# The address offset between activations and weight buffers in a two-layer decoder kernel: 112 bytes for every activation slot

## The chip, the cores and the metric

The kernel runs on one core of a Trainium2 chip. The metric is device time in microseconds for one execution. A core has a matrix engine (PE; its weight loads are listed apart as PEld), a vector engine (DVE), a scalar engine (ACT), a general engine (POOL) and queues that issue transfers (SP). All tiles below lie in the core's on-chip memory, which has 128 partitions; an address is a byte position inside a partition.

## What is computed

A decoder trunk of two layers over 256 tokens with model width 2048. Cut to its lines of work:

```
u = rms_norm(h, mix_norm[0]);  q, f, i, g = split(u @ w_a_in, 4)       # layer 0: gated linear recurrence
h += (head_norm(recurrence(q, f, i)) * silu(g)) @ w_a_out
u = rms_norm(h, mix_norm[1]);  q = u @ w_b_q                           # layer 1: forgetting attention
h += (softmax(q k^T / sqrt(d) + D_t - D_s) v) @ w_b_out
# behind the mixer of either layer:
h += relu(rms_norm(h, mlp_norm) @ w_up)**2 @ w_down                    # d_ff = 8192
h += (p @ w_ple_up) * sigmoid(rms_norm(h, ple_norm) @ w_ple_gate)
# behind layer 0: k, v, f = split(rms_norm(h, kv_norm) @ w_kvf)
out = rms_norm(h, final_norm)
```

Everything is float32. Nearly all of the work is matrix products of 256 tokens with weights of 2048 rows.

## The kernel before

**Precision.** A float32 number is split into two numbers of the matrix engine's single-pass float32 format: a high part (a rounding copy) and a low part (the rest). A product is three matmuls: high weight with high activation, high weight with low activation, low weight with high activation.

**Weights.** `load_slab` (L78) brings 1 MB of weights into one of three `raw` buffers, with a transfer issued from the SP queue. ACT writes the high parts into one of four `whi` buffers (L92), DVE the low parts into one of four `wlo` buffers (L93). A `whi` or `wlo` buffer is 4096 bytes a partition.

**Two kinds of product.** In `mm_split` (L105, called by `mm_tile`) the weights are the stationary operand, a block of 128x128, and the activations are the moving operand, 256 columns: L111, L112 and L113 are its three matmuls, and 16 steps over the contraction make 48 matmuls for an output block `ps`. In `mm_tokens` (L116) it is the other way round: a block of activations is stationary and 512 or 416 columns of weights move (L130 to L132). It serves only the values of the recurrence (stationary `u_a`, 512 columns) and the values of the attention (stationary `u_kv`, 416 columns).

**Activations.** They live in three large slots, each with 16 x 2 x 256 float32 a partition: 16 blocks of the contraction, high and low part, 256 tokens. A step of the contraction is 2048 bytes and a part 1024 bytes, so all blocks of a slot start at the same place modulo 256 bytes. A step in the weight buffers is 512 bytes. `shifted` (L68) allocates a slot a little larger than needed and begins the data some elements into it. The embeddings' tile `pt` is made by the same helper. Who uses which slot, in the order of the program:

| slot | tiles |
|---|---|
| A | `u_a`, `hid` of layer 0 in chunks 0 and 2, `u_kv`, `u_m` of layer 1, `u_p` of layer 1 |
| B | `o_a`, `hid` of layer 0 in chunks 1 and 3, `u_q`, `hid` of layer 1 in chunks 0 and 2 |
| C | `u_m` and `u_p` of layer 0, `o_b`, `hid` of layer 1 in chunks 1 and 3 |

**Stages, in order of time.** Recurrence: `u_a` with the weights of forget gate, query and gate, and small matmuls for each of 16 heads between blocks of 48. Output projection: `o_a`. MLP: `up(0)`, then `up(b)`, `down(b-1)` for four chunks b, each with 16 blocks of 48, that is 768 matmuls; `up` moves `u_m`, `down` moves `hid`. Embedding stage (`ple`): 16 blocks with `u_p`, and 6 matmuls with `pt` for each. Then the attention with `u_kv` (values, keys) and `u_q` (queries), its projection with `o_b`, and MLP and embedding stage again. A framework puts the instructions of an engine in order from the program's text and a simulated timeline, and an allocator gives the addresses.

Of the kernel before, what the change touches and what calls it, by code (L numbers as in the profile page):

```python
# [11 lines left out]
F32R = mybir.dt.float32r  # L12
# [6 lines left out]
P = 128  # L19
T = 256  # L20
D = 2048
KC = D // P
# [12 lines left out]
def yoco_kernel(ctx, tc, a, out):  # L35
    nc = tc.nc
    big = ctx.enter_context(tc.tile_pool(name="big", bufs=1))
# [27 lines left out]

    h = big.tile([P, KC, T], F32, name="h", tag="h")

    def shifted(pool, kc, name, tag, bufs=None):  # L68

        n = kc * 2 * T  # L70
        t = pool.tile([P, n + 16], F32R, name=name, tag=tag, bufs=bufs or 1)
        return t[:, 12 : 12 + n].rearrange("p (k w t) -> p k w t", w=2, t=T)

    def slot(which, name):
        return shifted(big, KC, name, "slot" + which)


    def load_slab(src, n, parts, before=None):  # L78

        raw = wp.tile([P, D], F32, name="raw", tag="raw", bufs=3)  # L80
        m = n // parts
        if not before:
            nc.sync.dma_start(raw[:, :n], src)
        got = []
        for i in range(parts):
            r = raw[:, i * m : (i + 1) * m]
            if before:
                before[i]()
                nc.sync.dma_start(r, src[:, i * m : (i + 1) * m])
            hi = wp.tile([P, 1024], F32R, name="whi", tag="whi", bufs=4)  # L90
            lo = wp.tile([P, 1024], F32R, name="wlo", tag="wlo", bufs=4)
            nc.scalar.copy(hi[:, :m], r)  # L92
            nc.vector.tensor_tensor(lo[:, :m], r, hi[:, :m].bitcast(F32), op=ALU.subtract)  # L93
            got.append((hi, lo))
        return got
# [4 lines left out]
    def mm_tile(src, act, kcs=KC):  # L100

        pairs = load_slab(src, kcs * P, 2 if kcs > 8 else 1)
        return mm_split(pairs, act, kcs)

    def mm_split(pairs, act, kcs=KC, off=0):  # L105
        ps = psm.tile([P, T], F32, name="ps", tag="mm")
        for k in range(kcs):
            kk = k + off
            pair, kl = pairs[kk // 8], kk % 8
            st, sp = k == 0, k == kcs - 1  # L110
            nc.tensor.matmul(ps, wk(pair, kl, 0), act[:, k, 0, :], start=st, stop=False)  # L111
            nc.tensor.matmul(ps, wk(pair, kl, 0), act[:, k, 1, :], start=False, stop=False)  # L112
            nc.tensor.matmul(ps, wk(pair, kl, 1), act[:, k, 0, :], start=False, stop=sp)  # L113
        return ps
# [70 lines left out]
    def plain_split(dst, k, src):  # L185
        nc.scalar.copy(dst[:, k, 0, :], src)
        nc.vector.tensor_tensor(dst[:, k, 1, :], src, dst[:, k, 0, :].bitcast(F32), op=ALU.subtract)
# [11 lines left out]
    def mlp(layer, u, stats, slots, u2, g2, pool):  # L199
# [3 lines left out]
        def up(b):  # L203
            hid[b] = slot(slots[b % 2], f"hid{layer}_{b}")
            for n in range(KC):
                ps = mm_tile(a["w_up"][layer, b * KC + n], u)
                if not rs:
                    rs.append(stats.rstd())
                t = pool.tile([P, T], F32, name="up", tag="up", bufs=2)
                nc.vector.scalar_tensor_tensor(t, ps, 0.0, rs[0], op0=ALU.max, op1=ALU.mult)  # L210
                s = pool.tile([P, T], F32, name="hsq", tag="hsq", bufs=2)
                nc.scalar.activation(s, t, AF.Square)
                plain_split(hid[b], n, s)
# [18 lines left out]
    def ple(layer, u, stats, after, pool):  # L232

        praw = pool.tile([P, 2, T], F32, name="praw", tag="praw", bufs=1)
        nc.gpsimd.dma_start(praw, a["pT"][layer])
        pt = shifted(pool, 2, "pt", "pt")
        for k in range(2):
            plain_split(pt, k, praw[:, k, :])
        rstd = None
        wu = None  # L240
        for n in range(KC):
            if n % 8 == 0:
                wu = load_slab(a["w_pu"][layer, n // 8], D, 2)
            pu = mm_split(wu, pt, kcs=2, off=2 * (n % 8))
            up = pool.tile([P, T], F32, name="up", tag="up", bufs=2)
            nc.scalar.copy(up, pu)
            last = layer == 1 and n == KC - 1
            ps = mm_tile(a["w_pg"][layer, n], u)
            rstd = rstd or stats.rstd()
            t = pool.tile([P, T], F32, name="gate", tag="gate", bufs=2)  # L250
            nc.vector.tensor_tensor(t, ps, rstd, op=ALU.mult)
            s = pool.tile([P, T], F32, name="sig", tag="sig", bufs=2)
            nc.scalar.activation(s, t, AF.Sigmoid)
            if last:

                nc.scalar.activation(scrap, s[:, 0:1], AF.Sqrt)
            nc.vector.tensor_tensor(up, up, s, op=ALU.mult)
            nc.vector.tensor_tensor(h[:, n, :], h[:, n, :], up, op=ALU.add)
            after(n)
# [14 lines left out]
    nc.vector.tensor_scalar(nomlb, omlb, -1.0, None, op0=ALU.mult)  # L274

    u_a = slot("A", "u_a")
    o_a = slot("B", "o_a")
    with tc.tile_pool(name="hg", bufs=2) as hp, tc.tile_pool(name="hps", bufs=1, space=PSUM) as hps:

# [251 lines left out]
    late = ctx.enter_context(tc.tile_pool(name="late", bufs=1))  # L531

    def slotc(name):
        return shifted(late, KC, name, "slotC")

    _slot = slot

    def slot(which, name):
        return slotc(name) if which == "C" else _slot(which, name)
# [21 lines left out]
    def after0(n):  # L561
        scaled_split(u_kv, n, G_KV)
        scaled_split(u_q, n, G_MIX + 1)
        st_kv.add(n)

    ple(0, up_(), stats, after0, mp)
    mctx.__exit__(None, None, None)

# [130 lines left out]
    def after1(n):  # L699
        st_f.add(n, n == KC - 1)  # L700
        nc.scalar.activation(h[:, n, :], h[:, n, :], AF.Copy, scale=gains[:, G_FIN, n : n + 1])

    ple(1, up_(), stats, after1, mp)
    rstd = st_f.rstd()
    k = 0
# [69 lines left out]
```

## Time and profile before

| | |
|---|---|
| time, median of 3 runs | 2541.58 us (2541.26 to 2541.87) |
| profiled execution | 2541.92 us, of which its span is 2539.8 us |
| granted clock of the matrix engine | 0.998 |
| busy: PE, DVE, ACT, POOL | 99%, 62%, 51%, 1% |
| matmuls in the profile | 20808 |
| weights and other data read | 464.35 MB, 184 GB/s over the span |

The span runs from the first to the last instruction; about 2 us of the time lie outside it. A matmul's recorded duration is longer than the distance to the next one, since matmuls are pipelined: where the text speaks of the pitch, it is that distance, from start to start, found as the length of a stretch divided by its number of matmuls. In tables by stretches each row gives start and end, then the length, then for each engine busy time and number of instructions; PEclk is the granted clock as a share of full speed.

### The profile page before, as it was taken

The page shows a single profiled execution, that of the slowest core. Times are in us where ns is not written, and L with a number is a line of the kernel's source. Part 1 is how long each engine was busy: PE and PEld are TensorE (multiplying, and loading weights), DVE is VectorE, ACT ScalarE, POOL GpSimd, SP SyncE. Part 2 cuts the span into 40 slices and gives each one's busy share as a digit, 9 for nine tenths or more (in the row PEclk, how much of TensorE's full clock was granted, in tenths as well). Part 3 has the DMA queues.
Part 4 walks back from the last instruction along what each step waited for, and adds up shares of the span by engine and source line. Part 5 has one row for each costly group of instructions (what it writes and reads, how often), then busy time and mean ns, then how long its engine had stood idle before and what let it go on. Part 6 is the DMA issues. An engine that isn't in the chain of part 4 may idle for free.

```text
span 2539.8 us, 48653 instructions
## 1 busy us (share of the span) xinstructions
PE 2523.9 (99%) x20808; PEld 2501.8 (99%) x20808; DVE 1569.9 (62%) x2350; ACT 1284.7 (51%) x1966; POOL 23.8 (1%) x71
## 2 busy tenths in 40 slices
PE   9999999999999999999999999999999999999997
PEld 8999999999999999999999999999999999999997
DVE  8787787655545555556774566665555555555665
ACT  7665565545434434445654555555443443444554
POOL 1000000000000000000000000000000000000000
PEclk9999999999999999999999999999999999999999
DMA  6455455555555555555555555555555555555553
GB/s 250 166 175 188 170 174 196 191 190 185 183 183 186 196 187 190 188 183 198 185 175 191 192 172 172 179 189 185 183 185 198 184 185 190 190 184 199 183 183 117
DMA packets 68505, 469.62 MB, mean 185 GB/s; under 512 B 7936, under 2 KB 8640, under 8 KB 15040
## 3 DMA queue, kind: packets, MB, share of 16 engines
q1 hardware_dynamic: 66096, 460.88, 52.3%
q0 software_dynamic: 1760, 4.78, 1.0%
q8 instruction: 163, 2.67, 0.4%
q10 hardware_dynamic: 432, 0.85, 0.1%
q14 instruction: 54, 0.44, 0.0%
HBM read 464.35 MB, written 2.13 MB: 184 GB/s over the span
## 4 chain that ended last, share of the span: by engine, by line
PE 99%; ACT 0%; DVE 0%; DMA 0%; SPq 0%; DVEq 0%; issue 0%
PE ps L111 30%; PE ps L112 30%; PE ps L113 30%; PE pst L131 2%; PE pst L132 2%; PE pst L130 2%; PE pa L437 0%; PE pl L638 0%; DMA h<-in_xT 0%; PE ptp L661 0%; DVE h L708 0%; PE ms L474 0%; PE pob L671 0%; PE pb L440 0%; PE po L459 0%; PE pa L439 0%
## 5 line engine op out<-in xcount | busy, mean ns | idle before, releaser
L93 DVE TENSOR_TENSOR wlo<-raw,whi 128x1024 fp32r<-128x1024 f32 (+2 forms) x882 | 1069.2, 1213 | 706.5 <-ACT whi L92 705.3
L92 ACT CAST whi<-raw 128x1024 fp32r<-128x1024 f32 (+2 forms) x882 | 917.6, 1041 | 1157.4 <-PE ps L112 1006.1
L111 PE MATMUL ps<-u_m,whi 128*128 128x256 f32 x2048 | 575.6, 281 | 0.0
L113 PE MATMUL ps<-u_m,wlo 128*128 128x256 f32 x2048 | 575.3, 281 | 0.0
L112 PE MATMUL ps<-u_m,whi 128*128 128x256 f32 x2048 | 575.3, 281 | 0.0
L111 PE MATMUL ps<-hid,whi 128*128 128x256 f32 x2048 | 569.3, 278 | 0.0
L112 PE MATMUL ps<-hid,whi 128*128 128x256 f32 x2048 | 569.3, 278 | 0.0
L113 PE MATMUL ps<-hid,wlo 128*128 128x256 f32 x2048 | 569.3, 278 | 0.0
L112 PEld LDWEIGHTS ps<-u_m,whi 128*128 128x128 f32 x2048 | 384.9, 188 | 0.1
L111 PEld LDWEIGHTS ps<-u_m,whi 128*128 128x128 f32 x2048 | 384.9, 188 | 0.1
L113 PEld LDWEIGHTS ps<-u_m,wlo 128*128 128x128 f32 x2048 | 384.9, 188 | 0.0
L112 PEld LDWEIGHTS ps<-hid,whi 128*128 128x128 f32 x2048 | 384.6, 188 | 0.0
L111 PEld LDWEIGHTS ps<-hid,whi 128*128 128x128 f32 x2048 | 384.6, 188 | 0.0
L113 PEld LDWEIGHTS ps<-hid,wlo 128*128 128x128 f32 x2048 | 384.6, 188 | 0.0
L111 PE MATMUL ps<-u_a,whi 128*128 128x256 f32 x768 | 217.6, 283 | 0.0
L113 PE MATMUL ps<-u_a,wlo 128*128 128x256 f32 x768 | 216.7, 282 | 0.0
L112 PE MATMUL ps<-u_a,whi 128*128 128x256 f32 x768 | 216.1, 281 | 0.0
L111 PEld LDWEIGHTS ps<-u_a,whi 128*128 128x128 f32 x768 | 144.5, 188 | 0.2
L112 PEld LDWEIGHTS ps<-u_a,whi 128*128 128x128 f32 x768 | 144.5, 188 | 0.2
L113 PEld LDWEIGHTS ps<-u_a,wlo 128*128 128x128 f32 x768 | 144.4, 188 | 0.0
L112 PE MATMUL ps<-u_p,whi 128*128 128x256 f32 x512 | 143.7, 281 | 0.0
L111 PE MATMUL ps<-u_p,whi 128*128 128x256 f32 x512 | 143.7, 281 | 0.0
(257 smaller groups left out, 3674.3 us busy)
## 6 DMA issues: line engine op xcount, KB each, us to landing
raw<-in_w_up SPq DMA_DIRECT2D x128, 1024.0 KB, 4.9
raw<-in_w_down SPq DMA_DIRECT2D x128, 1024.0 KB, 4.8
raw<-in_w_ain SPq DMA_DIRECT2D x48, 1024.0 KB, 4.8
raw<-in_w_pg SPq DMA_DIRECT2D x32, 1024.0 KB, 4.9
raw<-in_w_vf SPq DMA_DIRECT2D x20, 832.0 KB, 4.4
raw<-in_w_aout SPq DMA_DIRECT2D x16, 1024.0 KB, 4.7
raw<-in_w_k SPq DMA_DIRECT2D x16, 1024.0 KB, 4.7
raw<-in_w_q SPq DMA_DIRECT2D x16, 1024.0 KB, 6.4
```

The costliest lines, as they stand in the source:

```text
L92: nc.scalar.copy(hi[:, :m], r)
L93: nc.vector.tensor_tensor(lo[:, :m], r, hi[:, :m].bitcast(F32), op=ALU.subtract)
L111: nc.tensor.matmul(ps, wk(pair, kl, 0), act[:, k, 0, :], start=st, stop=False)
L112: nc.tensor.matmul(ps, wk(pair, kl, 0), act[:, k, 1, :], start=False, stop=False)
L113: nc.tensor.matmul(ps, wk(pair, kl, 1), act[:, k, 0, :], start=False, stop=sp)
L130: nc.tensor.matmul(o, act[:, kk, 0, tok], hi, start=st, stop=False)
L131: nc.tensor.matmul(o, act[:, kk, 0, tok], lo, start=False, stop=False)
L132: nc.tensor.matmul(o, act[:, kk, 1, tok], hi, start=False, stop=sp)
```

## The change

All slots and `pt` get more room, and their data begin at another place in it, so that they start 112 bytes past a multiple of 256 bytes counted from the weight buffers.

```diff
-    def shifted(pool, kc, name, tag, bufs=None):
+    def shifted(pool, kc, name, tag, shift):
         n = kc * 2 * T
-        t = pool.tile([P, n + 16], F32R, name=name, tag=tag, bufs=bufs or 1)
-        return t[:, 12 : 12 + n].rearrange("p (k w t) -> p k w t", w=2, t=T)
+        t = pool.tile([P, n + 64], F32R, name=name, tag=tag, bufs=1)
+        return t[:, shift : shift + n].rearrange("p (k w t) -> p k w t", w=2, t=T)
     def slot(which, name):
-        return shifted(big, KC, name, "slot" + which)
+        return shifted(big, KC, name, "slot" + which, 60)
...
-        pt = shifted(pool, 2, "pt", "pt")
+        pt = shifted(pool, 2, "pt", "pt", 28)
...
     def slotc(name):
-        return shifted(late, KC, name, "slotC")
+        return shifted(late, KC, name, "slotC", 28)
```

The shift counts elements of 4 bytes. The addresses of the two programs, as allocated:

| | first byte before | mod 256 | past the weights | first byte after | mod 256 | past the weights |
|---|---|---|---|---|---|---|
| `whi` (4 buffers) | 131456 | 128 | | 131840 | 0 | |
| `wlo` (4 buffers) | 147840 | 128 | | 148224 | 0 | |
| slot A | 32944 | 176 | 48 | 33136 | 112 | 112 |
| slot B | 65776 | 240 | 112 | 66160 | 112 | 112 |
| slot C | 164272 | 176 | 48 | 164720 | 112 | 112 |
| `pt` | 203248 | 240 | 112 | 203888 | 112 | 112 |

"Past the weights" is the difference of the two places modulo 256. The residual stream `h` stays where it was; the constants and the `raw` buffers move up by 384 bytes like the weights, the working tiles of the recurrence too, and those of the MLP and the attention by 576. No instruction is added, removed or moved: on each engine the order, the shapes and the waits are the same in both programs.

## The prediction

> **What bounds the kernel now.** I read the page's busy times and chain first, then the waits of PE.
>
> ```profile
> span 2539.8 us, 48653 instructions
> PE 2523.9 (99%) x20808; PEld 2501.8 (99%) x20808; DVE 1569.9 (62%) x2350; ACT 1284.7 (51%) x1966; POOL 23.8 (1%) x71
> PE 99%; ACT 0%; DVE 0%; DMA 0%; SPq 0%; DVEq 0%; issue 0%
> ```
> ```profile
> PE ps_ssq L161 <- ACT sq L148: 2.4, 1, 2.4
> PE warm L56 <- POOL ones L52: 1.1, 1, 1.1
> PE pst L131 <- DVE wlo L93: 0.8, 2, 0.5
> PE pst L130 <- ACT whi L92: 0.7, 2, 0.5
> ```
>
> The chain of work that ended last is PE for 99% of the span, and the four rows are all that PE waited for: 5.0 us. So the time is the number of matmuls times their pitch, and only a change of the pitch can move it. The next view asks whether the pitch is the same everywhere: the `down` steps of the two MLPs, tile `hid`, one row for each.
>
> ```profile
> core 0: us, PE busy (x) PEld busy (x) DVE busy (x) ACT busy (x), PEclk, DMA share, GB/s
> 673.30:764.20 90.90, 90.89 (x768) 90.84 (x768) 0.42 (x1) 0.41 (x1) 1.00 0.54 186
> 855.10:942.20 87.10, 87.10 (x768) 87.02 (x768) 0.42 (x1) 0.41 (x1) 1.00 0.56 193
> 1033.00:1123.90 90.90, 90.86 (x768) 90.90 (x769) 0.42 (x1) 0.41 (x1) 1.00 0.53 185
> 1123.90:1211.00 87.10, 87.10 (x770) 87.07 (x768) 0.00 (x0) 0.00 (x0) 1.00 0.56 193
> 1884.60:1971.70 87.10, 87.10 (x768) 87.03 (x768) 0.42 (x1) 0.41 (x1) 1.00 0.56 192
> 2062.50:2153.40 90.90, 90.85 (x768) 90.88 (x768) 0.42 (x1) 0.41 (x1) 1.00 0.54 185
> 2244.30:2331.40 87.10, 87.09 (x769) 87.10 (x770) 0.42 (x1) 0.41 (x1) 1.00 0.56 193
> 2331.40:2422.30 90.90, 90.90 (x770) 90.83 (x768) 0.00 (x0) 0.00 (x0) 1.00 0.54 187
> ```
>
> These eight steps do the same work with the same code at the same clock (1.00), yet four take 90.9 us and four take 87.1 us. By the table of slots those of 90.9 us use, in order, A, A, C, C, and those of 87.1 us B each time. A and C begin 48 bytes past the weights, B 112. The pitch is 90.9/768 = 118.4 ns at 48 and 87.1/768 = 113.4 ns at 112: a difference of 3.8 us for 768 matmuls, or 4.95 ns each. The same split shows in the recorded durations of one of the three matmuls by tile (least, median, most; first and last start).
>
> ```profile
> L112 PE MATMUL ps<-u_a,whi x768: 278/281/366, 31.1 to 403.8; 128*128 128x256 f32 x192
> L112 PE MATMUL ps<-u_m,whi x2048: 278/281/283, 491.2 to 2244.1; 128*128 128x256 f32 x187
> L112 PE MATMUL ps<-u_p,whi x512: 278/280/286, 1211.8 to 2524.6; 128*128 128x256 f32 x171
> L112 PE MATMUL ps<-u_kv,whi x256: 278/281/283, 1405.0 to 1601.5; 128*128 128x256 f32 x128
> L112 PE MATMUL ps<-u_q,whi x256: 275/275/281, 1412.2 to 1608.0; 128*128 128x256 f32 x128
> L112 PE MATMUL ps<-o_b,whi x256: 278/280/365, 1609.0 to 1702.2; 128*128 128x256 f32 x128
> ```
>
> Medians of 280 and 281 belong to tiles in A and C, 275 to `u_q`, which lies in B. Nothing else about a tile sorts them: `u_kv` and `u_q` alternate block by block in the same stage and still differ. A and C are far apart (32944 and 164272) and agree.
>
> **The change part by part.** It removes and adds no instruction and changes no wait; every price is a pitch.
>
> *Moving operands from A and C.* Each kind of product has three lines with the counts quoted above. `u_m`: 3 x 2048 = 6144 matmuls, 8 blocks of 768, all at 48 now: 8 x 3.8 = 30.4 us. `hid`: the four steps of 90.9 us, 4 x 3.8 = 15.2 us; the other four stay. `u_p`: 3 x 512 = 1536, 2 x 3.8 = 7.6 us. `o_b`: 768, one block with a few small matmuls in its first part: 3.7 us.
>
> *The stages with small matmuls in between.* The faster rhythm does not begin at once. PE's timeline at the first query block, three of its rows with seven left out between each two:
>
> ```profile
> 1412.16 0.28 PE L112 MATMUL ps<-u_q,whi 128*128 128x256 f32 x1
> ...
> 1413.10 0.28 PE L111 MATMUL ps<-u_q,whi 128*128 128x256 f32 x1
> ...
> 1414.01 0.28 PE L113 MATMUL ps<-u_q,wlo 128*128 128x256 f32 x1
> ```
>
> The first eight steps take 0.94 us, 117.5 ns each; the next eight take 0.91 us, 113.8 ns: about nine matmuls of a run go by before it is fast. In the recurrence each of 16 heads is interrupted twice (scores, outputs), so 32 runs lose 9 matmuls each: of `u_a`'s 3 x 768 = 2304, 2016 gain 4.95 ns, 10.0 us. `u_kv` has 16 runs: 768 - 144 = 624 gain, 3.1 us. Without that loss these would be 11.4 and 3.8 us, and if such runs gained nothing, 0; I take the counted value, since the row is of the same kind of block.
>
> *The embeddings' tile.* `pt` is at 112 already, but its six matmuls stand between those of `u_p`. PE's timeline at the first six of each layer, and the matmul behind them:
>
> ```profile
> 1211.00 0.28 PE L111 MATMUL ps<-pt,whi 128*128 128x256 f32 x1
> ...
> 1211.68 0.28 PE L111 MATMUL ps<-u_p,whi 128*128 128x256 f32 x1
> ```
> ```profile
> 2422.28 0.28 PE L111 MATMUL ps<-pt,whi 128*128 128x256 f32 x1
> ...
> 2422.98 0.28 PE L111 MATMUL ps<-u_p,whi 128*128 128x256 f32 x1
> ```
>
> Behind `hid` in B the six take 0.68 us, 113.3 ns each; behind `hid` in C 0.70 us, 116.7 ns. So a tile at 112 keeps a fast rhythm that it inherits, although it lies at 203248, far from B. With all neighbours at 112, the 2 x 16 x 6 = 192 matmuls gain about 4.95 ns each: 0.9 us.
>
> *Products with stationary activations.* Here the slot feeds the weight loads and the weights move, so the difference goes from -48 to -112, a relation that no stretch of the trace shows. The present pitch, for 512 columns from the chain in order of time (first and last of five such rows, 12 matmuls apart each), for 416 from the stretch of the attention's values:
>
> ```profile
> 17.14 0.47 PE pst L130 x2
> ...
> 28.34 0.47 PE pst L130 x2
> ```
> ```profile
> 1313.50:1404.60 91.10, 91.10 (x487) 90.36 (x486) 45.64 (x50) 43.64 (x55) 1.74 (x5) 1.00 0.55 188
> ```
>
> That is 11.20/48 = 233.3 ns, and 91.10/480 = 189.8 ns at most. Per column both are 0.456 ns, between 113.4/256 = 0.443 and 118.4/256 = 0.462. If they went to 0.443, 512 columns would take 226.8 ns (6.5 less, x384 = 2.5 us) and 416 columns 184.3 (5.5 less, x480 = 2.6 us): -5.1 us. If they went to 0.462, +3.3 x 384 + 2.4 x 480 = +2.4 us. I take 0, as they are near the middle, and keep -5.1 and, since the relation is new and could be worse than any seen, three times the loss, +7.
>
> *What hides the rest.* DVE and ACT read and write the shifted tiles too; they lie beside PE, and their cover must hold when PE is faster. The recurrence is the tightest stage, the projection behind it shows the fast pace:
>
> ```profile
> 31.00:404.00 373.00, 373.00 (x2887) 360.45 (x2886) 298.30 (x667) 233.76 (x477) 4.26 (x8) 1.00 0.51 177
> 404.00:491.10 87.10, 87.10 (x770) 87.10 (x769) 58.57 (x83) 45.58 (x66) 0.54 (x1) 1.00 0.56 195
> ```
> ```profile
> ACT whi L92 <- PE ps L112: 1006.1, 651, 3.9
> ```
>
> At 113.4 ns `o_a` is fed at 195 GB/s without a gap in PE. Over the kernel ACT waited 1006.1 us for PE to give back a weight buffer: conversion runs ahead. In the recurrence DVE is busy 298.30 of 373.00 us; at 363.0 us that is 82%. So no late feeder is costed.
>
> *Sum.* 30.4 + 15.2 + 7.6 + 3.7 + 10.0 + 3.1 + 0.9 = 70.9 us. The profiled execution took 2541.92 us (2539.8 in its span and 2.1 around it, which stays), so 2471.0; the median of the runs is 0.34 below it, so 2470.7 us.
>
> **The rivals.**
>
> *Absolute places (slower).* Before, the weights were always at 128 modulo 256, so the trace cannot tell the difference of 112 from B's own place, 240. The change puts the weights at 0 and the slots at 112, a place no slot had. If the place itself decides and 112 is like 176, A and C gain nothing and B's blocks fall to 90.9 us: `o_a`, four `hid` steps and `u_q`, 6 x 3.8 = 22.8 us, 2564.4. It decides if the pitch of `o_a` after is above 118. Against it: 240 and 112 are both 112 past a multiple of 128, while 176 is 48 past one, so a rule by places would have to need the full 256 bytes. For it: no row has weights at 0.
>
> *The change does nothing it says.* B could be fast for where it lies in the memory, between A and the weights; then all stays: 2541.6. For it: all 768-blocks at 113.4 are in B. Against it: `pt` at 203248, which stayed at 113.3.
> The Trainium skill, page "TensorE: Matmul & The Clock Gate", section "Step-by-step: what each phase is for", says that the engine has two independent read ports, so that loading the next tile's weights takes no read bandwidth from the running matmul. By that rule the distance between weights and activations could not matter, and the time would be that of this rival; 118.4 against 113.4 ns at one clock and one shape do not fit the rule alone, and no row says which mechanism stands behind it.
>
> *A feeder becomes the bound.* If DVE's chains hold the recurrence at its 373.0 us, its 10.0 us are lost: 2480.7. For it: DVE's 80% there. Against it: PE had no wait in that stage.
>
> **How the numbers follow.** The forecast holds with 0.84, the late feeder with 0.06, the change without effect with 0.04, absolute places with 0.06. The forecast's own range is 2470.7 - 5.1 to 2470.7 + 7, with some 3 us for the runs of 48: 2462 to 2481; with the late feeder, which lies inside once its end is moved to 2482, it holds more than 8 in 10. Faster by over 0.2% (5 us; about what a measurement of this kernel can tell from no change) are the first two cases, 0.90; within it the third, 0.04; slower the last, 0.06.
>
> **What would show it.** Right: all eight `hid` steps at 87.1 us; medians of 275 ns for `u_a`, `u_m`, `u_p`, `u_kv` and `o_b`; PE's waits still about 5 us. Wrong: `hid` steps that still come in two lengths (the region rival), `o_a` above 118 ns (absolute places), PE waiting for `wlo` in the first 400 us (feeder), or the 12-matmul step of the token products far from 2.80 us.

## The result and the profile after

The changed kernel takes 2472.22 us (median of 4 runs, 2471.91 to 2472.69) against 2541.46 us before (4 runs): a ratio of 0.9728, interval 0.9711 to 0.9744. The profiled execution took 2472.09 us, 69.8 us less than the one before; 70.9 us less were forecast.

The page's head, then all waits of PE, in the profile of the changed kernel (lines behind `shifted` stand one lower in its text, so L112 to L114 are the matmuls that were L111 to L113):

```profile
span 2470.0 us, 48653 instructions
PE 2453.6 (99%) x20808; PEld 2431.0 (98%) x20808; DVE 1568.3 (63%) x2350; ACT 1286.1 (52%) x1966; POOL 23.1 (1%) x71
PE 99%; DVE 0%; ACT 0%; DMA 0%; issue 0%; SPq 0%; DVEq 0%
```
```profile
PE ps_ssq L162 <- ACT sq L149: 2.4, 1, 2.4
PE pst L132 <- DVE wlo L94: 1.1, 2, 0.6
PE warm L56 <- POOL ones L52: 1.1, 1, 1.1
PE pst L131 <- ACT whi L93: 0.8, 1, 0.8
```

PE is still the whole chain, has as many matmuls, and waited 5.4 us instead of 5.0. Only its pitch moved. The eight `down` steps, tile `hid`, by stretches (four of them left out):

```profile
656.70:743.80 87.10, 87.06 (x768) 87.05 (x768) 0.42 (x1) 0.41 (x1) 1.00 0.56 195
830.80:917.90 87.10, 87.08 (x768) 87.03 (x768) 0.42 (x1) 0.41 (x1) 1.00 0.56 195
...
2008.80:2095.80 87.00, 87.00 (x768) 86.96 (x768) 0.42 (x1) 0.41 (x1) 1.00 0.56 193
...
2269.90:2356.90 87.00, 87.00 (x770) 86.98 (x768) 0.00 (x0) 0.00 (x0) 1.00 0.57 194
```

These are slots A, B, C and C. All eight now take 87.0 or 87.1 us, where before A and C took 90.9. The same kind of view stage by stage, behind the first 31 us, first after and then the rows of before that the prediction did not show:

```profile
30.90:395.10 364.20, 364.20 (x2887) 350.68 (x2886) 296.77 (x667) 234.07 (x477) 4.27 (x8) 1.00 0.50 181
395.10:482.10 87.00, 87.00 (x770) 87.00 (x769) 58.59 (x84) 45.61 (x66) 0.54 (x1) 1.00 0.56 198
482.10:1179.00 696.90, 696.90 (x6149) 696.85 (x6149) 402.60 (x480) 329.64 (x418) 0.00 (x0) 1.00 0.56 194
1179.00:1277.50 98.50, 98.50 (x868) 98.42 (x867) 79.19 (x128) 65.27 (x116) 0.00 (x0) 1.00 0.54 188
1277.50:1368.80 91.30, 91.30 (x488) 90.72 (x488) 45.98 (x50) 43.69 (x55) 1.76 (x5) 1.00 0.55 188
1368.80:1570.00 201.20, 201.20 (x1737) 200.14 (x1735) 124.80 (x220) 105.29 (x191) 9.15 (x17) 1.00 0.58 183
1570.00:1660.10 90.10, 90.10 (x793) 90.00 (x793) 59.26 (x89) 48.18 (x75) 0.54 (x1) 1.00 0.54 185
1660.10:2356.90 696.80, 696.80 (x6148) 696.75 (x6147) 402.59 (x480) 329.63 (x418) 0.00 (x0) 1.00 0.56 194
2356.90:2470.00 113.10, 99.75 (x872) 98.89 (x870) 73.73 (x105) 60.42 (x104) 0.00 (x0) 0.95 0.44 153
```
```profile
491.10:1211.00 719.90, 719.90 (x6148) 719.85 (x6147) 402.47 (x480) 328.86 (x418) 0.00 (x0) 1.00 0.54 188
1211.00:1313.50 102.50, 102.50 (x868) 102.45 (x867) 79.36 (x129) 65.16 (x116) 0.00 (x0) 1.00 0.53 182
...
1404.60:1608.80 204.20, 204.20 (x1738) 203.12 (x1736) 125.08 (x220) 105.41 (x191) 9.12 (x17) 1.00 0.56 180
1608.80:1702.40 93.60, 93.60 (x793) 93.50 (x793) 59.34 (x89) 48.08 (x75) 0.54 (x1) 1.00 0.53 180
1702.40:2422.30 719.90, 719.90 (x6149) 719.85 (x6148) 402.48 (x480) 328.82 (x418) 0.00 (x0) 1.00 0.55 188
2422.30:2539.80 117.50, 104.17 (x872) 102.99 (x870) 73.75 (x105) 60.83 (x104) 0.00 (x0) 0.95 0.42 147
```

The gain is spread as the slots are used (lengths before less lengths after): 8.8 us in the recurrence, 0.1 in its projection (slot B), 23.0 and 23.1 in the two MLPs, 4.0 and 4.4 in the embedding stages, 3.0 in keys, queries and softmax, 3.5 in the projection from C; the attention's values lose 0.2.

### The profile page after: what moved, and what is told of

Its sections match the earlier page's. It is cut to its first block, busy times and chain, and to the rows that moved or that the text cites. A ratio compares the mean times of both kernels' runs of the same rounds, so it can differ in the third digit from the quotient of the medians.

```text
span 2470.0 us, 48653 instructions
## 1 busy us (share of the span) xinstructions
PE 2453.6 (99%) x20808; PEld 2431.0 (98%) x20808; DVE 1568.3 (63%) x2350; ACT 1286.1 (52%) x1966; POOL 23.1 (1%) x71
## 4 chain that ended last, share of the span: by engine, by line
PE 99%; DVE 0%; ACT 0%; DMA 0%; issue 0%; SPq 0%; DVEq 0%
PE ps L114 30%; PE ps L112 30%; PE ps L113 30%; PE pst L132 2%; PE pst L133 2%; PE pst L131 2%; PE pa L438 0%; PE pl L639 0%; PE ptp L662 0%; DMA h<-in_xT 0%; DVE h L709 0%; PE po L459 0%; PE ms L475 0%; PE pb L442 0%; PE pob L672 0%; PE pob L673 0%
## 5 line engine op out<-in xcount | busy, mean ns | idle before, releaser
L112 PE MATMUL ps<-u_m,whi 128*128 128x256 f32 x2048 | 563.6, 275 | 0.0
L114 PE MATMUL ps<-u_m,wlo 128*128 128x256 f32 x2048 | 563.3, 275 | 0.0
L113 PE MATMUL ps<-u_m,whi 128*128 128x256 f32 x2048 | 563.3, 275 | 0.0
L112 PE MATMUL ps<-hid,whi 128*128 128x256 f32 x2048 | 563.2, 275 | 0.0
L113 PE MATMUL ps<-hid,whi 128*128 128x256 f32 x2048 | 563.2, 275 | 0.0
L114 PE MATMUL ps<-hid,wlo 128*128 128x256 f32 x2048 | 563.2, 275 | 0.0
L112 PEld LDWEIGHTS ps<-u_m,whi 128*128 128x128 f32 x2048 | 384.5, 188 | 0.1
L113 PEld LDWEIGHTS ps<-u_m,whi 128*128 128x128 f32 x2048 | 384.5, 188 | 0.1
L114 PEld LDWEIGHTS ps<-u_m,wlo 128*128 128x128 f32 x2048 | 384.4, 188 | 0.0
L112 PEld LDWEIGHTS ps<-hid,whi 128*128 128x128 f32 x2048 | 384.4, 188 | 0.0
L113 PEld LDWEIGHTS ps<-hid,whi 128*128 128x128 f32 x2048 | 384.4, 188 | 0.0
L114 PEld LDWEIGHTS ps<-hid,wlo 128*128 128x128 f32 x2048 | 384.4, 188 | 0.0
L112 PE MATMUL ps<-u_a,whi 128*128 128x256 f32 x768 | 214.0, 279 | 0.0
L114 PE MATMUL ps<-u_a,wlo 128*128 128x256 f32 x768 | 213.1, 277 | 0.0
L113 PE MATMUL ps<-u_a,whi 128*128 128x256 f32 x768 | 212.3, 276 | 0.0
L112 PEld LDWEIGHTS ps<-u_a,whi 128*128 128x128 f32 x768 | 144.3, 188 | 0.2
L113 PEld LDWEIGHTS ps<-u_a,whi 128*128 128x128 f32 x768 | 144.3, 188 | 0.2
L114 PEld LDWEIGHTS ps<-u_a,wlo 128*128 128x128 f32 x768 | 144.3, 188 | 0.0
L112 PE MATMUL ps<-u_p,whi 128*128 128x256 f32 x512 | 140.8, 275 | 0.0
L113 PE MATMUL ps<-u_p,whi 128*128 128x256 f32 x512 | 140.7, 275 | 0.0
```

## The experiments

The theory was that the pitch hangs on the distance between slots and weight buffers. Its rivals were the place in itself and the region of the memory. The first kernel separates these, six more draw the curve of pitch over distance, and the last ones ask what a single misplaced buffer does, whether a block inherits its pitch, and whether the token products have something to gain. All start from the changed kernel. Each kernel ran once, but for the last two; nine runs of the kernel before, taken beside those two, lie within 1.2 us of each other. A block is 768 matmuls; 87.1 us are 113.4 ns, 90.9 us 118.4 ns.

**Weights moved, slots kept.** A tile of 64 bytes goes ahead of the weight buffers, and the slots behind them begin 64 bytes earlier in their room, so that every slot keeps its address modulo 256.

```diff
+    pad = wp.tile([P, 16], F32, name="pad", tag="pad")
     h = big.tile([P, KC, T], F32, name="h", tag="h")
...
-        pt = shifted(pool, 2, "pt", "pt", 28)
+        pt = shifted(pool, 2, "pt", "pt", 12)
...
-        return shifted(late, KC, name, "slotC", 28)
+        return shifted(late, KC, name, "slotC", 12)
```

> The weight and raw buffers move up by 64 bytes, the three slots and pt stay at the places of the changed kernel (112 modulo 256); so every slot begins 48 bytes past the weights. Theory of the relation: all blocks of 768 matmuls take 90.9 us again, B's too: 2472.2 + 70.9 + 22.8 = about 2565 us. Rival of absolute places: nothing that moves has changed its place, so 87.1 us a block and about 2472 us. Rival of the region (B good for where it lies): B's four down steps at 87.1 us, A's and C's at 90.9, about 2542 us.

It took 2563.76 us. The first four of its eight `hid` steps, A, B, A, B (the other four have 90.9 us too):

```profile
677.00:767.90 90.90, 90.87 (x768) 90.87 (x768) 0.42 (x1) 0.41 (x1) 1.00 0.55 185
858.80:949.70 90.90, 90.90 (x768) 90.83 (x768) 0.42 (x1) 0.41 (x1) 1.00 0.54 186
1040.60:1131.40 90.80, 90.80 (x768) 90.80 (x769) 0.42 (x1) 0.41 (x1) 1.00 0.55 186
1131.40:1222.30 90.90, 90.90 (x770) 90.87 (x768) 0.00 (x0) 0.00 (x0) 1.00 0.54 185
```

The activations lie exactly where they do in the changed kernel, and all gain is gone, with B's old advantage. So neither the slots' own place nor the region decides. That it is the distance, and not the weights' own place, follows with the kernel before and the next one: 48 past the weights, slots at 176 (weights at 128), 112 (weights at 64) and 48 (weights at 0) modulo 256 all have 90.8 or 90.9 us, and 112 past them, slots at 240 (weights at 128) and 112 (weights at 0) both have 87.0 or 87.1.

**Other distances, three in each kernel.** Only the shifts differ: in the first of these A gets 32 elements, B 44 and C 16, which is 0, 48 and 64 bytes past the weights.

```diff
-        return shifted(big, KC, name, "slot" + which, 60)
+        return shifted(big, KC, name, "slot" + which, {"A": 32, "B": 44}[which])
...
-        return shifted(late, KC, name, "slotC", 28)
+        return shifted(late, KC, name, "slotC", 16)
```

> Slot A 0, B 48, C 64 bytes past the weights (weights as in the changed kernel). Theory of the relation: B's down steps and o_a take 90.9 us (118.4 ns), at least 22.8 us lost through B; A at 0 and C at 64 are open, since no run shows them: if the two streams clash when they start close together, 0 is the worst of the three. Rival of the region: B stays at 87.1 us.

> Slot A 128, B 176, C 240 bytes past the weights. If the relation repeats every 128 bytes, B (176 = 48 + 128) has 90.9 us for 768 matmuls, C (240 = 112 + 128) 87.1 us, and A the pitch that 0 gives. If it repeats only every 256 bytes, B and C differ from these. Rival of the region: B at 87.1 us whatever C does.

> Slot A 80, B 96, C 160 bytes past the weights. If the pitch falls steadily with the distance (120.0 ns at 0, 118.3 at 48, 117.8 at 64, 113.3 at 112 so far), A and B lie between 117.8 and 113.3 ns. If 112 stands in a narrow window, A and B stay at 117 to 120 ns. C at 160 lies between 128 (118.7 or 120.0) and 176 (119.3): 118.5 to 120. With all three slots at 117 to 120 the kernel takes 2550 to 2570 us.

> Slot A 208, B 32, C 144 bytes past the weights. B at 32 lies between 120.0 ns (at 0) and 118.3 ns (at 48); C at 144 between 118.7 and 119.3; A at 208 between 119.3 (176) and 117.1 (240). For the products with stationary u_a the weights begin 48 bytes past the slot here: if these follow the same table by the distance of the moving behind the stationary operand, they lie where 48 lies; at 0 they took 228.4 ns, at every other distance 232 to 235.

> Slot A 224, B 16, C 192 bytes past the weights. If the whole upper half of the 256 bytes is like 128 to 240, all three take 117 to 120 ns and nothing reaches 113.3. If there is a second window as good as 112, or one better than it, 192 or 224 shows it, since 128 to 176 and 240 are known.

> Slot A 120, B 104, C 124 bytes past the weights: the neighbourhood of 112 in steps of two and three elements. If the memory is read in lines of 16 bytes or more and only the line counts, 120 and 124 are as good as 112 (113.3 ns), and 104 as 96. If the exact distance counts, 120 and 124 stand between 113.3 and the 118.7 to 120.0 of 128.

The lengths of the blocks of `hid`, read as above, with the pitch that follows from them (length/768):

| kernel: A, B, C | time, us | A: us, ns | B: us, ns | C: us, ns |
|---|---|---|---|---|
| 0, 48, 64 | 2568.12 | 92.2, 120.1 | 90.9, 118.4 | 90.5, 117.8 |
| 128, 176, 240 | 2565.01 | 92.2 and 91.1, 120.1 and 118.6 | 91.6, 119.3 | 89.9, 117.1 |
| 80, 96, 160 | 2573.56 | 90.9 and 92.1, 118.4 and 119.9 | 92.2, 120.1 | 91.1 and 90.1, 118.6 and 117.3 |
| 208, 32, 144 | 2562.71 | 91.5, 119.1 | 89.6 and 90.5, 116.7 and 117.8 | 91.1 and 89.6, 118.6 and 116.7 |
| 224, 16, 192 | 2530.97 | 90.9, 118.4 | 89.6, 91.1 and 87.0; 116.7, 118.6 and 113.3 | 87.1, 113.4 |
| 120, 104, 124 | 2600.99 | 92.2 and 93.8, 120.1 and 122.1 | 92.2, 120.1 | 92.1, 119.9 |

The sharpest row is the last: with slots 8 bytes past 112 (A), 8 short of it (B) and 12 past it (C), no `hid` block is below 92.1 us. Its first three `hid` steps (A, B, A):

```profile
683.00:775.20 92.20, 92.17 (x768) 92.16 (x768) 0.42 (x1) 0.41 (x1) 1.00 0.54 183
867.40:959.50 92.10, 92.10 (x768) 92.08 (x768) 0.42 (x1) 0.41 (x1) 1.00 0.54 183
1050.00:1143.80 93.80, 93.80 (x768) 93.80 (x769) 0.42 (x1) 0.41 (x1) 1.00 0.52 181
```

So the idea of a pitch that falls steadily from 0 to 112 fell: for these blocks 112 is a narrow point, with some 120 ns on either side. The relation does not repeat every 128 bytes either: 176 is not 48 (119.3 against 118.4 ns), and 240 is not 112 (117.1 against 113.4). A distance can also have more than one pitch in one kernel. At 192, C's `u_m` blocks of layer 0 behind the first one:

```profile
582.20:669.20 87.00, 87.00 (x770) 86.97 (x768) 0.00 (x0) 0.00 (x0) 1.00 0.56 194
760.10:847.20 87.10, 87.10 (x768) 87.02 (x768) 0.00 (x0) 0.00 (x0) 1.00 0.56 193
936.80:1027.20 90.40, 90.40 (x768) 90.37 (x768) 0.00 (x0) 0.00 (x0) 1.00 0.55 187
```

Two are as short as at 112, the third is not. No distance tried was below 86.9 us for a block. At 192 both `hid` blocks had 87.1 us as well, but 112 is the only distance at which every block of 768 without a break in it, of `u_m` too, had 87.0 or 87.1.

**Only the low weights moved.** The 64-byte tile goes between `whi` and `wlo`, with the same shifts for C and `pt` as in the first experiment: the slots stay 112 past `whi` and are 48 past `wlo`.

```diff
+    padded = []
...
+            if not padded:
+                padded.append(wp.tile([P, 16], F32, name="pad", tag="pad"))
             lo = wp.tile([P, 1024], F32R, name="wlo", tag="wlo", bufs=4)
```

> Only the wlo buffers move up by 64 bytes: slots are 112 past whi and 48 past wlo. If each weight load clashes by its own distance with the activations that move meanwhile, one matmul in three takes 118.4 ns instead of 113.4: 115.1 ns, 88.4 us for 768, and the whole kernel about 2472.2 + 25 x 1.3 = 2504 us. If one late load upsets the rhythm of all three, all take 118.4 ns: 90.9 us a block and about 2565 us. If only the distance to whi counts, 2472 us.

It took 2559.07 us. The first and last `hid` steps:

```profile
672.50:763.80 91.30, 91.30 (x768) 91.25 (x768) 0.42 (x1) 0.41 (x1) 1.00 0.54 185
...
2350.30:2441.60 91.30, 91.30 (x770) 91.24 (x768) 0.00 (x0) 0.00 (x0) 1.00 0.54 184
```

All eight have 91.3 us (91.30/768 = 118.9 ns), more than the 90.9 us with both kinds of weights at 48. By the matmuls' starts in the first of them, the three lines take 121, 117 and 118 ns from start to start: here one load in three at another distance takes the gain from all three matmuls, and the price by single loads (88.4 us) is wrong. One block of the same kernel comes close to that price, though, `o_a`, in slot B at the same distances:

```profile
400.60:489.60 89.00, 88.97 (x768) 88.97 (x768) 0.42 (x1) 0.40 (x1) 1.00 0.55 191
```

Behind its first 64 matmuls its three lines take 118.3, 113.3 and 115.0 ns. So one pair of distances has two rhythms here as well, and why `o_a` got the shorter one is not shown.

**Is a pitch inherited?** A and B at 112, C at 64, by shifts of 60, 60 and 16 elements.

> Slots A and B 112, C 64 bytes past the weights. In the run with A at 0 and B at 48, C at 64 took 117.8 ns in most blocks of 768 and 113.3 ns in one of them. If a block inherits the rhythm of the one ahead of it wherever its own distance can carry it, the C blocks that follow an A or B block without a break (u_m in up(1) to up(3) of layer 0, hid in layer 1) run at 113.3 ns here, and only those behind a break may take 117.8: between 2472 and 2485 us. If the distance alone sets the pitch, seven or eight C blocks of 768 take 90.5 us instead of 87.1: 2472.2 + 8 x 3.4 = about 2499 us.

It took 2499.45 us. The last four `hid` steps, B, C, B, C:

```profile
1854.70:1941.70 87.00, 87.00 (x768) 86.99 (x768) 0.42 (x1) 0.41 (x1) 1.00 0.57 193
2028.80:2119.20 90.40, 90.40 (x768) 90.37 (x768) 0.42 (x1) 0.41 (x1) 1.00 0.55 187
2206.30:2293.30 87.00, 87.00 (x769) 87.00 (x769) 0.42 (x1) 0.41 (x1) 1.00 0.57 195
2293.30:2383.80 90.50, 90.50 (x770) 90.41 (x768) 0.00 (x0) 0.00 (x0) 1.00 0.55 188
```

C does not inherit B's 113.3 ns, and the time is that of the rule by distance alone (about 2499 us). What made single blocks at 16, 64 or 192 differ is not settled. It is not the pitch of the block ahead: in the kernel 0, 48, 64 two blocks of C behind B's 90.9 or 90.8 us took 86.9 (`u_m`) and 90.5 us (`hid`), and in the kernel 224, 16, 192 two `hid` blocks of B behind a `u_m` block of 90.9 us took 89.6 and 87.0.

**The token products at distance 0.** With the slot at 0 the recurrence's products of 512 columns had the shortest recorded durations (median of the first of the three matmuls 389 ns, 394 in the changed kernel); the kernel with the slot at 120 has 389 ns too. So that their distance is 0 with the slots at 112, their weights were put 28 elements into the buffers, with four parts of a slab instead of two, and the 416 columns at a step of 448. The edits inside the two helpers are left out below. The changed kernel ran again beside it.

```diff
-            return mm_tokens(lambda q: a["w_av"][grp, q], u_a, 512)
+            return mm_tokens(lambda q: a["w_av"][grp, q], u_a, 512, parts=4, off=28)
...
-            pv = mm_tokens(lambda q: a["w_vf"][g, q], u_kv, VC)
+            pv = mm_tokens(lambda q: a["w_vf"][g, q], u_kv, VC, off=28, pitch=448)
```

> The changed kernel with the token products put at distance 0 as well: their weights begin 112 bytes into the buffers (the values of the recurrence in four parts instead of two from the second group on, the 416 columns of the attention's values at a step of 448, so that every block has the same distance). Slots stay at 112 past the weights for all other products. By the 228.4 ns that 512 columns took with the slot at 0, 288 x 6.2 ns = 1.8 us less; if 416 columns follow in proportion (228.4 x 416/512 = 185.6 ns instead of 188.8), 480 x 3.2 = 1.5 us less: 2468.9 us. If twice as many conversions of half the size make the recurrence wait, or the 448 step breaks another rhythm: 2472 to 2480 us.

> The changed kernel once more, beside the one with the token products moved: 2472.2 us within 0.5 us, so that the two can be compared on the same chip.

It took 2469.33 us (4 runs, 2468.97 to 2469.57; ratio to before 0.9716, interval 0.9702 to 0.9729), the changed kernel 2472.20 us (5 runs, 2471.52 to 2472.36; 0.9727, 0.9713 to 0.9740). No run of the one lies among those of the other, though the intervals of the ratios overlap. By stages, recurrence and attention's values, the new kernel first:

```profile
30.70:393.50 362.80, 362.80 (x2888) 350.11 (x2886) 298.81 (x688) 238.92 (x500) 4.26 (x8) 1.00 0.51 180
1275.90:1366.40 90.50, 90.50 (x488) 90.06 (x487) 45.94 (x50) 43.76 (x55) 1.72 (x5) 1.00 0.57 191
```
```profile
30.70:394.80 364.10, 364.10 (x2887) 350.62 (x2886) 296.77 (x667) 234.04 (x477) 4.26 (x8) 1.00 0.52 181
1277.30:1368.60 91.30, 91.30 (x489) 90.69 (x488) 45.97 (x50) 43.74 (x55) 1.75 (x5) 1.00 0.57 190
```

The values gain 0.8 us, where 1.5 were expected (their 480 products, from start to start, went from 90.6 to 89.8 us); distance and step changed together there, so which of them it was is not shown. The recurrence gains 1.3, where 1.8 were expected. These 1.3 us do not come from the distance. From start to start the recurrence's 288 token products take 67.8 us in this stage, 67.6 in the changed kernel, and where 20 or more of them run without a break their pitch is 230 to 233 ns, against 227 in the kernel with the slot at 0. So distance 0 did not bring that pitch back: for products with stationary activations the rule by distance is not confirmed. What fell are `u_a`'s other matmuls, by 1.0 us, and the small ones, by 0.4: with four parts the matmuls stand in another order, and `u_a`'s come in 43 uninterrupted runs instead of 53.

## Why the prediction was right

*Reading.* Eight steps of one code at one clock with two lengths, sorted by one table of addresses, gave both the mechanism and its price. Moving the weights alone is the test the old trace could not make. It measured 2563.76 us, where the distance asked for about 2565, the places for about 2472 and the region for about 2542. The signs that the prediction named came true: all eight `hid` steps at 87.0 or 87.1 us, medians of 275 ns for `u_a`, `u_m`, `u_p`, `u_kv` and `o_b`, 5.4 us of waits, and 2.80 us for 12 token products (16.90 to 19.70 us).

*The sum, by its terms.* The MLPs: `u_m` 30.4 and `hid` 15.2 make 45.6 us; 46.1 measured. The embedding stages: 7.6 and 0.9 make 8.5; 8.4 measured. `o_b`: 3.7; 3.5 measured. `u_kv`: 3.1; 3.0 measured. `u_a`: 10.0; 8.8 measured over its stage, the one term that was clearly off. The stage's 1.2 us and 0.2 in the attention's values, less 0.5 that the MLPs gained beyond their term, make most of the difference between 70.9 and 69.8. The price of 9 matmuls at the head of a run came from a query block of the attention, and it about holds; the number of runs was wrong. By the starts in both traces `u_a`'s matmuls come in 53 runs, not 32, since `squares`, scores and outputs often stand apart: 1879 of 2303 recorded matmuls have a pitch below 114.5 ns after, where 2016 were counted. That leaves 424, or 8 for a run. Averaged over the runs the pitch is 118 ns from the fourth to the ninth matmul, 115.2 and 114.2 in the next two threes, and 113.3 or 113.4 from the sixteenth on. `u_a`'s own matmuls take 9.2 us less (275.7 to 266.5), and the small ones between them 0.3 us more.

*Token products.* Taken at 0 with bounds of -5.1 and +7, and 0 was measured: from start to start the 480 products of the attention take 90.6 us in both traces, and the 288 of the recurrence's stage 67.5 and 67.6.

*The late feeder.* It did not come: in the recurrence PE is busy for all of 364.20 us, with DVE at 296.77 (81%).

*The skill's rule.* The two independent read ports that the Trainium skill, page "TensorE: Matmul & The Clock Gate", section "Step-by-step: what each phase is for", gives the engine would by the prediction's reading have left the time at 2541.6 us. Two kernels in which the large products differ in the places of the weights alone, 2563.76 against 2472.22 us, do not agree with that reading, that a weight load never slows the moving operand.

*What was lucky.* Against the rival of places the prediction said that 240 and 112 are both 112 past a multiple of 128, so that a rule by places would need the full 256 bytes. That was no good argument: the rule that holds does need them, as 240 and 176 past the weights are not like 112 and 48. The prediction also did not know how exact the distance has to be. It copied B's 112 to the byte, and that was needed: the kernel with its slots at 120, 104 and 124 takes 2600.99 us, more than the kernel before.

## What to carry to other kernels

Where the matrix engine is the whole chain, compare the lengths of equal blocks that use different buffers: in this kernel a difference at one clock and one shape was an address effect, and its price per block gave the price of the change. Then measure the distance between stationary and moving operands by moving one of them alone, and try exact values, since neighbours of a good one can be worse than average. Put all slots and all weight buffers, high and low, on one good distance, and check it again whenever an allocation ahead of either changes size. Do not carry the distance over to products with stationary activations: the one test of it on them failed here.

## What the runs showed of the hardware that was not expected

- The pitch of a 256-column matmul moved from 113.3 to 122.1 ns (87.0 to 93.8 us for 768) with nothing but the shifts of the slots against the weights.
- The best distance is narrow to a few elements: at 104, 120 and 124 the `hid` blocks took 92.1 us or more, at 112 they took 87.1.
- With a third of the weight loads at 48 and the others at 112 the `hid` blocks cost more (91.3 us) than with all of them at 48 (90.9 us), while `o_a` cost 89.0 us.
- At 16, 32, 64, 80, 120, 128, 144, 160 and 192 blocks of one kernel had different lengths at the same distance; at 48 and 112 the `hid` blocks of all kernels with `whi` and `wlo` alike had one. At 64 one `u_m` block of four had 86.9 us, in the kernel with A at 0:

```profile
586.60:677.10 90.50, 90.50 (x771) 90.50 (x769) 0.00 (x0) 0.00 (x0) 1.00 0.55 188
769.40:859.70 90.30, 90.30 (x768) 90.30 (x768) 0.00 (x0) 0.00 (x0) 1.00 0.54 186
950.70:1037.60 86.90, 86.90 (x767) 86.90 (x768) 0.00 (x0) 0.00 (x0) 1.00 0.57 192
```

What inside the memory or the engine makes a distance good was not shown, nor what chooses among the lengths that one distance can have; the runs tell only which distances are good.
